# Hybrid decoder step on one core: the low part of the keys meets only the high part of the queries, two heads at a time

## The chip, the cores and the metric

The kernel runs on one core of one Trainium2 chip. The metric is the device time of one execution in microseconds (us); lower is better. Three executions of the kernel before took 1845.82, 1846.70 and 1847.45 us, so its median is 1846.7 us. Engines are called TensorE (PE in the profile, its weight loads PEld), VectorE (DVE), ScalarE (ACT), GpSimd (POOL) and SyncE (SP).

## The reference, cut to what matters

The reference is one layer of a decoder trunk for 1024 prompt tokens and 8 new tokens (1032 rows in all). All numbers are float32. The two steps that the change touches are these:

```
# the indexer, per 128-query block: 8 heads of 64, one shared key of 64
logits = einsum("bqhd,bld->bqhl", qi, ki_all)
score  = einsum("bqhl,bqh->bql", relu(logits), wi)
score  = where(key position <= query position, score, -inf)
idx    = top_k(score, 256)

# attention over the chosen keys: 16 query heads, 4 key groups, 64 wide
s = einsum("bqcgd,bqkcd->bqcgk", q, k[idx])
p = softmax(where(valid, s, -inf))
o = einsum("bqcgk,bqkcd->bqcgd", p, v[idx])
```

Ahead of them stand an RMS norm and one wide input projection; beside them a gated spatial unit; behind them an output projection, a squared-ReLU MLP and a gated embedding.

## The kernel before, in words

**High and low parts.** TensorE multiplies in a rounded float32 type, one pass for each matmul. To keep precision, an operand x is split into a high part (rounded) and a low part (the rest), and a product takes several matmuls that add up in the same place. Dense projections take three (high by high, high by low, low by high). Scores are done otherwise. A head is 64 wide and the array has 128 rows, so `split_heads` stacks a query head's high part and low part into the 128 rows: for an even head the high part lies in rows 0 to 63 and the low part in rows 64 to 127, for an odd head the other way round. The keys' high part is laid twice, in both halves of the rows (`kih` for the indexer, `khd[c]` for key group c of attention), and so is their low part (`kil`, `kld[c]`). One matmul with the high keys then gives (high + low query) by high key, and a second with the low keys gives (high + low query) by low key.

**Index scores.** `score_tiles` goes over the query tiles 2 to 7 (tile i sees L = 128 (i + 1) keys; tiles 0 and 1 need no choice). For each of the 8 heads it takes a room of two banks (`bank2`, there are two such rooms, used in turn, and other steps of that phase use them too), makes the logits in stretches of at most 512 keys, lets ScalarE take the relu out of it, and VectorE adds it with its weight to the tile's score. It is a generator: `tick`, called after each group of a dense projection, advances it by one step, that is one head for tiles 4 to 7 and two heads for tiles 2 and 3. So score matmuls stand between groups of 24 dense matmuls on TensorE's in-order queue. VectorE meanwhile picks the 256 best of finished tiles in the background (`take_tiles`, maximum of 8 and replace), which `pump` paces by modelled clocks.

**Attention.** 32 units (8 query tiles by 4 key groups, in the order of `units`: a long and a short tile alternate) are given as operations with an engine, a planned duration, dependencies and a priority (`Op`); `emit` plays them through with these durations and writes them to the engines' queues in the order that results. For a unit of L keys there are: scores on TensorE (tile "sc"; before, one operation for each head if L > 512, one for two heads otherwise, where the two heads share one room of two banks), a masked copy with the row's maximum on VectorE for each head (`masked`), the exponential on ScalarE, transposes of the probabilities on TensorE in steps of 128 keys (tile "pp"), their copy on ScalarE or VectorE, and the product with the values on TensorE (tile "po", two matmuls side by side on 64 columns of the array each). `s_used` keeps the last masked copy of each score operation; a score operation waits for the one before the last, whose room it takes over.

The change touches `score_tiles` and, within `unit_ops`, `scores` and the loop that makes the score operations. The planned duration of a score operation was 0.85 L + 15 ns for each head.

Of the kernel before, what the change touches and what calls it, by code (L numbers as in the profile page):

```python
# [16 lines left out]
P = 128  # L17
# [23 lines left out]
LAT, LAT2, SLACK, S_FIRST, T_LAST = 180.0, 60.0, 0.0, 1.5, 0.1  # L41
# [28 lines left out]
def step_kernel(ctx, tc, xT, pT, w_in, w_o, w_up, w_down, w_pg, w_p, gv, gqk, wsT, b_s,  # L70
# [35 lines left out]
    def slot(name, shape=(P, T), dt=F32):  # L106
        return big.tile(list(shape), dt, name=name, tag="s", bufs=NSLOT)
# [13 lines left out]
    def bank2(name):  # L121
        return ps.tile([P, 1024], F32, name=name, tag="big", bufs=2)

    mm = pe.matmul
# [222 lines left out]
    for k in range(KC):  # L347
        h, l = slot("xh", dt=F32R), slot("xl", dt=F32R)
# [25 lines left out]
    qis = [qis_all[:, h, :] for h in range(HI)]  # L374
# [68 lines left out]
    kih, kil = key_split  # L443
# [5 lines left out]
    def mask_tile(i):  # L449
        L = (i + 1) * P  # L450
        if i not in (2, 4):
            return slot("mask", [P, L])
        if not packs:
            packs[0] = slot("mask", [P, 1024])
        return packs[0][:, :L] if i == 2 else packs[0][:, 1024 - L:]

    def score_tiles(tiles):
        behind = None
        n = 0
        for i in tiles:  # L460
            L = (i + 1) * P
            mask[i] = m = mask_tile(i)
            for h in range(HI):
                p = bank2("lg")
                for a in range(0, L, 512):
                    b = min(L, a + 512)
                    mm(p[:, a:b], qis[h][:, i * P:(i + 1) * P], kih[:, a:b], start=True, stop=False)
                    mm(p[:, a:b], qis[h][:, i * P:(i + 1) * P], kil[:, a:b], start=False, stop=True)
                rl = slot("rl", [P, L])
                act.activation(rl, p[:, :L], AF.Relu)  # L470
                if behind:
                    behind()

                def behind(m=m, rl=rl, h=h, i=i, L=L):
                    if h == 0:
                        dve.tensor_scalar(m, rl, wi[:, i, h:h + 1], None, op0=ALU.mult)
                    else:
                        dve.scalar_tensor_tensor(out=m, in0=rl, scalar=wi[:, i, h:h + 1], in1=m,
                                                 op0=ALU.mult, op1=ALU.add)
                    if h == HI - 1:  # L480
                        pool.affine_select(out=m[:, L - P:], in_=m[:, L - P:], pattern=[[-1, P]],
                                           compare_op=ALU.is_ge, fill=FUTURE, base=0, channel_multiplier=1)
                        scored.add(i)
                n += 1
                if i > 3 or n % 2 == 0:
                    yield 1
        behind()
        yield 1
# [13 lines left out]
    def take_tiles(tiles):  # L502
# [12 lines left out]
        yield 1  # L515

    paced.append(score_tiles(range(2, NT)))
    pairs = [(a, a + 1) for a in range(2, NT, 2)]
    takers = {t: take_tiles(t) for t in pairs}
# [385 lines left out]
    khd, kld = {}, {}  # L905
# [8 lines left out]
    qsts = {}  # L914
# [102 lines left out]
    for a, b in GROUPS[NG:]:  # L1017
# [10 lines left out]
        def scaled(eng, a, b, rest):  # L1028
            rest["sg"] = part("sg")
            eng.tensor_tensor(out=rest["sg"], in0=rest["p"][:, :b - a], in1=R[:, a:b], op=ALU.mult)  # L1030

        def gate(eng, rest):
            eng.activation(rest["sg"], rest["sg"], AF.Tanh, scale=0.5)

        def times(eng, a, b, rest):
            eng.scalar_tensor_tensor(out=mx_last[:, a:b], in0=rest["sg"], scalar=1.0, in1=mx_last[:, a:b],
                                     op0=ALU.add, op1=ALU.mult)
# [3 lines left out]
        o = Op("DVE", 430.0, lambda e, a=a, b=b, rest=rest: scaled(e, a, b, rest), [prev], -9.0)  # L1041
        o = Op("ACT", 380.0, lambda e, rest=rest: gate(e, rest), [o], -9.0)
        o = Op("DVE", 430.0, lambda e, a=a, b=b, rest=rest: times(e, a, b, rest), [o], -9.0)
    gated_out = Op("Pool", 2300.0, lambda e: gate_out(NT - 1, u_last, mx_last), [o], -9.0)
    keys_ready = {0: None}
# [15 lines left out]
    units = [(order[n + h], c) for n in range(0, NT, 2) for c in range(HKV) for h in range(2)]  # L1061
    q_ops = {order[0]: [], order[1]: []}
    s_ops, s_used, t_ops, t_used, pv_ops, ends, lasts = [], [], [], [], [], [], []
    q_last = {}

    def query_ops(i, deps, prio):
# [2 lines left out]
    def unit_ops(n, i, c):  # L1069
        L = (i + 1) * P  # L1070
        cols = slice(i * P, (i + 1) * P)
        env = {"p": [], "pt": {}}
        per = 4 if L <= 256 else 2 if L <= 512 else 1
        prio = float(n)
        back2 = ends[n - 2] if n >= 2 else None
        back3 = ends[n - 3] if n >= 3 else None
        room = lasts[n - 3] if n >= 3 else None
# [5 lines left out]
        ld = Op("SP", 120.0, load, [back3, gated_out if c == HKV - 1 else None], prio, lag=3000.0)  # L1083

        def scores(eng, hs):
            room = bank2("sc")
            for n, h in enumerate(hs):
                p = env["sc", h] = room[:, 512 * n:] if n else room
                lhs = qsts[i][h % 2][:, 2 * c + h // 2, :]
                for a in range(0, L, 512):  # L1090
                    b = min(L, a + 512)
                    mm(p[:, a:b], lhs, khd[c][:, a:b], start=True, stop=False)
                    mm(p[:, a:b], lhs, kld[c][:, a:b], start=False, stop=True)

        def masked(eng, h):
            if h == 0:
                env["mx"], env["sum"] = small("mx4", [P, 8], bufs=4), small("sm4", [P, 4], bufs=4)
            if h % per == 0:
                env["room"] = slot("p", [P, per, L])
            s = env["room"][:, h % per, :]  # L1100
            env["p"].append(s)
            eng.tensor_tensor_reduce(out=s, in0=env["sc", h][:, :L], in1=mask[i], scale=1.0, scalar=FUTURE,
                                     op0=ALU.add, op1=ALU.max, accum_out=env["mx"][:, h:h + 1])

        def bias(eng, h):
            sc = s_q[:, 2 * c + h // 2, i, h % 2:h % 2 + 1]
            eng.scalar_tensor_tensor(out=env["mx"][:, 4 + h:5 + h], in0=env["mx"][:, h:h + 1], scalar=-1.0, in1=sc,
                                     op0=ALU.mult, op1=ALU.mult)

        def exponential(eng, h):  # L1110
            s = env["p"][h]
            sc = s_q[:, 2 * c + h // 2, i, h % 2:h % 2 + 1]
            eng.activation(s, s, AF.Exp, bias=env["mx"][:, 4 + h:5 + h], scale=sc, accum_out=env["sum"][:, h:h + 1])  # L1113

        exps = []
        some = 2 if L <= 512 else 1
        for h0 in range(0, 4, some):
            hs = range(h0, h0 + some)
            deps = q_ops[i] + [keys_ready[c], room, s_ops[-1] if s_ops else None,
                               s_used[-2] if len(s_used) >= 2 else None]  # L1120
            so = Op("PE", some * (0.85 * L + 15), lambda e, hs=hs: scores(e, hs), deps, prio - S_FIRST)
            s_ops.append(so)
            for h in hs:
                mo = Op("DVE", 1.06 * L + 60, lambda e, h=h: masked(e, h), [so, back3, taken.get(i)], prio)
                bo = Op("DVE", 75.0, lambda e, h=h: bias(e, h), [mo], prio)
                exps.append(Op("ACT", 1.06 * L + 240, lambda e, h=h: exponential(e, h), [bo], prio))
            s_used.append(mo)

        def inverse(eng):
            rc = small("rc4", [P, 4], bufs=2)  # L1130
            eng.reciprocal(rc, env["sum"])
            env["rx"] = small("rx", [P, 4, 64], bufs=1)
            eng.tensor_copy(env["rx"], rc.unsqueeze(2).to_broadcast([P, 4, 64]))
# [57 lines left out]
    for n, (i, c) in enumerate(units):  # L1191
        if i not in q_ops:
            query_ops(i, [lasts[n - 4]] if n >= 4 else [], n - 8.0)
        unit_ops(n, i, c)
# [195 lines left out]
    for f in range(FFB):  # L1390
        for j in range(2):
            row = 4 * j
            for q, c in enumerate((j, j + 2)):
                h = hw[:, row + q, :]
# [85 lines left out]
    for n, (f, o) in enumerate(steps):  # L1480
# [26 lines left out]
        a = Pair("pa", True)  # L1507
# [19 lines left out]
        c = Pair("pc", False)  # L1527
# [3 lines left out]
        b = Pair("pb", False)  # L1531
# [35 lines left out]
    for k in range(KC):  # L1567
        e = slot("e")
# [86 lines left out]
```

## Time and profile before

| | |
|---|---|
| median of three runs | 1846.7 us |
| the profiled execution | 1844.18 us |
| its span in the profile | 1842.5 us |
| TensorE busy, instructions | 1795.2 us, 12106 matmuls |
| VectorE busy | 1269.2 us |
| ScalarE busy | 703.6 us |
| GpSimd busy | 556.9 us |
| index scores (tile lg) | 160 matmuls, from 65.7 to 283.9 us |
| attention scores (tile sc) | 384 matmuls, from 680.5 to 905.6 us |

The profile is of one execution. A row of the timeline gives the start and the length of an instruction, or of several alike that follow each other. Matmuls overlap in the array: the length of one is longer than the distance to the next, so what a matmul costs in a stream is the distance between starts, called a step here. A weight load (PEld) belongs to each matmul. The form 128*128 ahead of the operand's shape is rows by columns of the array that the instruction uses. The end of a matmul is modelled.

### The profile page before, as it was taken

To read this page: it belongs to the slowest core of one execution; us is meant where nothing else is said; L and a number is where in the kernel's file an instruction comes from. 1 tells how busy PE (TensorE), PEld (TensorE's weight loads), DVE (VectorE), ACT (ScalarE), POOL (GpSimd) and SP (SyncE) were. 2 spreads that over 40 slices of the span, in tenths; PEclk is the share of its full clock that TensorE was granted. 3 is DMA by queue.
4 is the path that set the end of the run, shared out by engine and by line. 5 is a ranking of instruction groups with operands and counts; after the bars stand their busy time and mean duration, and the time that the engine had idled before them with its cause. 6 is when DMAs were issued, how large, how long until landed. Compare 5 with 4: busy or idle time off the path is not lost.

```text
span 1842.5 us, 30644 instructions
## 1 busy us (share of the span) xinstructions
PE 1795.2 (97%) x12106; PEld 1689.0 (92%) x12106; DVE 1269.2 (69%) x2330; ACT 703.6 (38%) x1248; POOL 556.9 (30%) x511
## 2 busy tenths in 40 slices
PE   8999989999999999999999999999999999999898
PEld 8998879999999996777699999999998999999798
DVE  7489978989977757777744455556564666767743
ACT  5554332145311127777722333333335211211521
POOL 4233354457332221101012212211132336632321
PEclk9999999999999999999999999999999999999999
DMA  4122132222222265133142365555645667754233
GB/s 173 52 103 104 58 111 85 98 93 91 75 71 91 81 162 124 41 87 98 43 162 97 116 213 207 207 207 210 213 163 189 257 257 293 259 210 172 102 114 117
DMA packets 127328, 258.32 MB, mean 140 GB/s; under 512 B 13192, under 2 KB 58128, under 8 KB 127184
## 3 DMA queue, kind: packets, MB, share of 16 engines
q1 hardware_dynamic: 124992, 251.63, 39.7%
q0 software_dynamic: 2048, 4.72, 0.9%
q8 instruction: 95, 1.56, 0.3%
q14 instruction: 49, 0.40, 0.1%
q10 hardware_dynamic: 144, 0.02, 0.0%
HBM read 166.32 MB, written 90.01 MB: 139 GB/s over the span
## 4 chain that ended last, share of the span: by engine, by line
PE 80%; DVE 7%; issue 4%; POOL 4%; ACT 3%; DMA 1%; SPq 0%; POOLq 0%; ACTq 0%; DVEq 0%
PE acc L64 51%; PE pa L64 4%; PE pd L64 4%; PE pc L64 4%; PE po L64 4%; PE sc L64 4%; PE pp L64 4%; DVE mask L64 2%; PE pb L64 2%; DVE m L64 1%; POOL wlo L196 1%; PE mix L64 1%; DVE qs L64 1%; DMA kib<-cache_ki,idx 1%; PE lg L64 1%
## 5 line engine op out<-in xcount | busy, mean ns | idle before, releaser
L64 PE MATMUL acc<-xh,whi 128*128 128x344 f32 (+1 forms) x1144 | 372.9, 329 | 3.4 <-DVE s_q L64 1.8
L64 PE MATMUL acc<-xh,wlo 128*128 128x344 f32 (+1 forms) x1144 | 365.1, 323 | 1.8 <-POOL r_x L271 1.1
L64 PE MATMUL acc<-xl,whi 128*128 128x344 f32 (+1 forms) x1144 | 365.0, 323 | 1.0 <-DVE xl L64 0.9
L64 PE MATMUL acc<-nh,whi 128*128 128x344 f32 x960 | 303.0, 321 | 1.1 <-ACT e L1348 1.1
L64 PE MATMUL acc<-nh,wlo 128*128 128x344 f32 x960 | 301.8, 320 | 0.0
L64 PE MATMUL acc<-nl,whi 128*128 128x344 f32 x960 | 301.5, 319 | 0.0
L64 PEld LDWEIGHTS acc<-xh,whi 128*128 128x128 f32 x1144 | 216.4, 190 | 12.1 <-issue 5.0
L64 PEld LDWEIGHTS acc<-xh,wlo 128*128 128x128 f32 x1144 | 216.0, 189 | 2.7 <-POOL r_x L271 1.5
L64 PEld LDWEIGHTS acc<-xl,whi 128*128 128x128 f32 x1144 | 216.4, 190 | 2.2 <-DVE xl L64 1.8
L64 PEld LDWEIGHTS acc<-nh,whi 128*128 128x128 f32 x960 | 179.3, 188 | 2.8 <-ACT e L1348 1.8
L64 PEld LDWEIGHTS acc<-nl,whi 128*128 128x128 f32 x960 | 179.5, 188 | 0.0
L64 PEld LDWEIGHTS acc<-nh,wlo 128*128 128x128 f32 x960 | 179.4, 188 | 0.0
L64 DVE MATCH_REPLACE8 mask<-m,mask 128x384 f32<-128x384 f32 (+2 forms) x192 | 166.6, 875 | 0.0
L196 POOL TENSOR_TENSOR wlo<-wraw,whi 128x1024 fp32r<-128x1024 f32 x47 | 113.5, 2415 | 157.7 <-ACT whi L195 96.6
L64 DVE MAX8 m<-mask 128x8 f32<-128x384 f32 (+2 forms) x192 | 161.0, 880 | 0.0
L64 DVE TENSOR_TENSOR hop<-hw,hop 128x516 fp32r<-128x516 f32 x112 | 90.3, 817 | 98.1 <-ACT hop L1302 98.0
L1399 POOL TENSOR_TENSOR hw<-z 128x344 f32<-128x344 f32 x96 | 72.9, 761 | 278.1 <-ACT z L1398 278.1
L1398 ACT ACTIVATE z<-z 128x344 f32<-128x344 f32 x96 | 47.0, 492 | 221.0 <-DVE z L64 221.0
L1113 ACT ACTIVATE p<-p,mx,s_q 128x1024 f32<-128x1024 f32 (+7 forms) x128 | 110.4, 865 | 22.6 <-DVE mx L64 21.9
L195 ACT CAST whi<-wraw 128x1024 fp32r<-128x1024 f32 x96 | 100.1, 1043 | 1.4 <-DMA wraw<-w_up 1.3
L64 DVE CUSTOM_DVE_ANT_0 p<-sc,mask 128x1024 f32<-128x1024 f32 (+5 forms) x96 | 83.5, 886 | 22.0 <-PE sc L64 20.9
L64 PE MATMUL sc<-kh,qst 128*128 128x512 f32 (+3 forms) x384 | 89.3, 361 | 2.4 <-DVE mx L64 2.4
(303 smaller groups left out, 3526.7 us busy)
## 6 DMA issues: line engine op xcount, KB each, us to landing
h_d<-hop SPq DMA_DIRECT2D x98, 516.0 KB, 3.1
hop<-h_d SPq DMA_DIRECT2D x98, 516.0 KB, 5.9
wraw<-w_in SPq DMA_DIRECT2D x48, 512.0 KB, 4.1
wraw<-w_up SPq DMA_DIRECT2D x32, 512.0 KB, 4.4
draw<-w_down SPq DMA_DIRECT2D x32, 512.0 KB, 5.4
q_d<-qs SPq DMA_DIRECT2D x16, 512.0 KB, 3.5
qst<-q_d SPq DMA_DIRECT2D x16, 512.0 KB, 5.6
x<-xT SPq DMA_DIRECT2D x15, 516.0 KB, 8.2
```

Source lines behind the costliest of these rows:

```text
L64: return fn(*args, **kw)
L195: act.copy(hi, raws[n])
L196: eng.tensor_tensor(out=lo, in0=raws[n], in1=hi.bitcast(F32), op=ALU.subtract)
L1113: eng.activation(s, s, AF.Exp, bias=env["mx"][:, 4 + h:5 + h], scale=sc, accum_out=env["sum"][:, h:h + 1])
L1398: act.activation(z, z, AF.Relu)
L1399: pool.tensor_tensor(out=h[:, a:b], in0=z, in1=z, op=ALU.mult)
```

## The change

A new helper `head_pair` makes the scores of two heads. It takes one room of two banks if L is at most 512 and both rooms otherwise. For each stretch of at most 512 keys it issues the two full matmuls with the high keys, one for each head. Then it issues two matmuls with the low keys that use 64 rows each: the even head's high part in rows 0 to 63, the odd head's high part in rows 64 to 127. The product of the queries' low part and the keys' low part is no longer made. `score_tiles` calls it at each even head and reads the second result at the odd head. In attention each score operation makes two heads at any L; one of more than 512 keys waits for the masked copies of both score operations before it, and one of at most 512 keys that follows a long one waits for that one's last masked copy too. The planned duration becomes 0.69 L + 15 ns for each head.

```diff
+    def head_pair(name, L, q, kh, kl):
+        room = bank2(name)
+        outs = [room, room[:, 512:] if L <= 512 else bank2(name)]
+        for a in range(0, L, 512):
+            b = min(L, a + 512)
+            for x in range(2):
+                mm(outs[x][:, a:b], q(x), kh[:, a:b], start=True, stop=False)
+            for x in range(2):
+                o = slice(64 * x, 64 * x + 64)
+                mm(outs[x][:, a:b], q(x)[o], kl[o, a:b], start=False, stop=True)
+        return outs
...
             for h in range(HI):
-                p = bank2("lg")
-                for a in range(0, L, 512):
-                    b = min(L, a + 512)
-                    mm(p[:, a:b], qis[h][:, i * P:(i + 1) * P], kih[:, a:b], start=True, stop=False)
-                    mm(p[:, a:b], qis[h][:, i * P:(i + 1) * P], kil[:, a:b], start=False, stop=True)
+                if h % 2 == 0:
+                    ps_ = head_pair("lg", L, lambda x: qis[h + x][:, i * P:(i + 1) * P], kih, kil)
+                p = ps_[h % 2]
...
+    both_rooms = []
...
         def scores(eng, hs):
-            room = bank2("sc")
-            for n, h in enumerate(hs):
-                p = env["sc", h] = room[:, 512 * n:] if n else room
-                lhs = qsts[i][h % 2][:, 2 * c + h // 2, :]
-                for a in range(0, L, 512):
-                    b = min(L, a + 512)
-                    mm(p[:, a:b], lhs, khd[c][:, a:b], start=True, stop=False)
-                    mm(p[:, a:b], lhs, kld[c][:, a:b], start=False, stop=True)
+            outs = head_pair("sc", L, lambda x: qsts[i][x][:, 2 * c + hs[0] // 2, :], khd[c], kld[c])
+            for h, p in zip(hs, outs):
+                env["sc", h] = p
...
-        some = 2 if L <= 512 else 1
-        for h0 in range(0, 4, some):
-            hs = range(h0, h0 + some)
-            deps = q_ops[i] + [keys_ready[c], room, s_ops[-1] if s_ops else None,
-                               s_used[-2] if len(s_used) >= 2 else None]
-            so = Op("PE", some * (0.85 * L + 15), lambda e, hs=hs: scores(e, hs), deps, prio - S_FIRST)
+        for h0 in range(0, 4, 2):
+            hs = range(h0, h0 + 2)
+            used = s_used[-2:] if L > 512 else s_used[-2:-1] + [u for u in s_used[-1:] if u in both_rooms]
+            deps = q_ops[i] + [keys_ready[c], room, s_ops[-1] if s_ops else None] + used
+            so = Op("PE", 2 * (0.69 * L + 15), lambda e, hs=hs: scores(e, hs), deps, prio - S_FIRST)
...
             s_used.append(mo)
+            if L > 512:
+                both_rooms.append(mo)
```

## Rows read from the trace of the kernel before

**Rows 1.** The page, busy time of TensorE: us, share of the span, instructions

```profile
PE 1795.2 (97%) x12106; PEld 1689.0 (92%) x12106; DVE 1269.2 (69%) x2330; ACT 703.6 (38%) x1248; POOL 556.9 (30%) x511
```

**Rows 2.** Windows: stretch, its length, busy us of each engine, clock, DMA share, GB/s

```profile
60.00:140.00 80.00, 79.64 (x513) 75.04 (x513) 58.30 (x112) 43.68 (x91) 22.91 (x15) 1.00 0.26 90
140.00:220.00 80.00, 72.98 (x459) 67.61 (x458) 78.62 (x168) 34.11 (x65) 28.67 (x17) 0.98 0.24 86
220.00:290.00 70.00, 60.99 (x357) 56.27 (x356) 54.11 (x97) 21.66 (x29) 39.86 (x48) 0.93 0.31 102
...
676.00:920.00 244.00, 238.88 (x1652) 170.57 (x1652) 183.48 (x568) 176.89 (x367) 26.04 (x35) 1.00 0.35 91
```

**Rows 3.** Waits (total us, times, longest) and groups of 676 to 912 us

```profile
DVE p L64 <- PE sc L64: 21.4, 30, 3.0
...
PEld sc L64 <- DVE mx L64: 4.8, 8, 1.6
...
L64 PE MATMUL sc<-kh,qst 128*128 128x512 f32 (+3 forms) x384 | 89.3, 361 | 2.4 <-DVE mx L64 2.4
L64 DVE CUSTOM_DVE_ANT_0 p<-sc,mask 128x1024 f32<-128x1024 f32 (+5 forms) x96 | 83.5, 886 | 22.0 <-PE sc L64 20.9 <-PE acc L64 0.7
```

**Rows 4.** Chain of waits, 640 to 960 us: start, us, what

```profile
709.05 0.93 PE sc L64 x4
...
739.68 0.63 PE sc L64 x4
...
814.71 0.70 PE sc L64 x4
...
851.94 0.82 PE sc L64 x4
```

**Rows 5.** Timeline of TensorE around 765.59 us: one, two and eight value matmuls

```profile
765.59 0.43 PE L64 MATMUL po<-pt,vt 128*64 128x256 f32 x1
...
765.59 0.44 PE L64 MATMUL po<-pt,vt 128*64 128x256 f32 x2
...
765.59 1.08 PE L64 MATMUL po<-pt,vt 128*64 128x256 f32 x8
```

**Rows 6.** Timeline of TensorE, 336.6 to 338.1 us: 64 rows between full matmuls

```profile
336.75 0.32 PE L64 MATMUL acc<-xh,wlo 128*128 128x344 f32 x1
337.00 0.70 PE L64 MATMUL dix<-dw,sel 64*128 64x257 f32 x2
...
338.04 0.32 PE L64 MATMUL acc<-xh,wlo 128*128 128x344 f32 x1
```

**Rows 7.** Timeline of TensorE, 384.5 to 385.5 us, and that tile's group

```profile
384.61 0.32 PE L64 MATMUL acc<-xh,wlo 128*128 128x344 f32 x1
384.76 1.03 PE L64 MATMUL dsc<-kb,zq 128*128 128x257 f32 x4
...
L64 PE MATMUL dsc<-kb,zq 128*128 128x257 f32 x32 | 8.4, 383 | 1.8 <-ACT kb L768 1.8
```

**Rows 8.** Timeline of TensorE, 60.8 to 62.3 us, and the last transpose's group

```profile
60.90 0.33 PE L64 MATMUL acc<-xh,wlo 128*128 128x388 f32 x1
61.16 0.77 PE L64 MATMUL wit<-ident,kraw 64*128 64x64 f32 x9
...
62.28 0.32 PE L64 MATMUL acc<-xh,wlo 128*128 128x344 f32 x1
...
L64 PE MATMUL wit<-ident,kraw 64*8 64x64 f32 x1 | 0.2, 216 | 0.0
```

**Rows 9.** Timeline of TensorE: the first and the last scores followed by values

```profile
694.90 1.18 PE L64 MATMUL sc<-kh,qst 128*128 128x512 f32 x4
696.01 0.87 PE L64 MATMUL po<-pt,vt 128*64 128x256 f32 x6
...
905.01 0.93 PE L64 MATMUL sc<-kh,qst 128*128 128x384 f32 x4 [0.15 <-DVE mx L64]
905.87 0.65 PE L64 MATMUL po<-pt,vt 128*64 128x256 f32 x4
```

**Rows 10.** Waits of 62 to 290 us: who waited for whom, total us, times, longest

```profile
PE lg L64 <- ACT rl L470: 7.0, 2, 5.0
...
PE hst L64 <- DVE qs L64: 4.5, 3, 1.7
```

## The prediction

> **What bounds the kernel now.** I read the shares of the page first. TensorE is busy for 97% of the span [rows 1], so any change of its work is suspect of moving the end. A busy share is a mean, so the windows come next, one for each stretch that the change touches [rows 2]. The index scores (tile "lg") lie between 60 and 290 us. From 60 to 140 us TensorE is busy 79.64 of 80 us and VectorE 58.30. From 140 to 220 us it is the other way round: VectorE 78.62, TensorE 72.98. From 220 to 290 us neither is full. The attention scores (tile "sc") lie in the stage from 676 to 920 us, where TensorE is busy 238.88 of 244 us, VectorE 183.48 and ScalarE 176.89. The groups and waits of that stage say the same: the 384 score matmuls are a large share of its TensorE time, VectorE waits 21.4 us in 30 waits for scores, and TensorE's weight loads wait 4.8 us in 8 waits for VectorE [rows 3]. So in the attention stage every microsecond of TensorE counts almost fully, in the index stage only partly.
>
> **What one step of a matmul costs.** The chain of waits shows runs of four score matmuls, two heads' worth of one pass pair, at four key lengths: 0.93 us at 1024 keys, 0.82 at 896, 0.70 at 768 and 0.63 at 640 [rows 4]. Each run is one head: two matmuls of 512 columns and two of the rest. So a step of 512 columns is 0.93/4 = 0.2325 us, and two of the rest cost 0.355, 0.235 and 0.165 us: 0.178 us a step at 384 columns, 0.118 at 256, 0.083 at 128. At 128 that is more than a quarter of the 512 step: there the weight load binds.
>
> **What goes.** Call a block what one pass of the new loop does: two heads, one stretch of up to 512 keys. Before, it is four full matmuls. After, it is two full ones, and two half ones, each on 64 of the array's 128 rows, meant to run side by side: the time of one. The number of instructions stays; one step a block goes, if the halves do run together. Attention: 4 key groups x 2 pairs x (one block for tiles 0 to 3, two for tiles 4 to 7) = 96 blocks, which fits the 384 matmuls of [rows 3]. 48 are 512 wide, 16 each 384, 256 and 128 wide: 48 x 0.2325 + 16 x (0.178 + 0.118 + 0.083) = 17.2 us. Index: 4 pairs of heads, tiles 2 to 7, 40 blocks, of which 24, 8, 4 and 4 have these widths: 5.6 + 1.4 + 0.5 + 0.3 = 7.8 us. The trace has no two halves by rows, but it has pairs by columns, the "po" matmuls on 64 of 128 columns: one takes 0.43 us, two together 0.44, and eight of 256 columns 1.08 us [rows 5], where eight one after another would take 8 x 0.217 = 1.74 (0.217 is the step of 257 such columns on the full array, below). So a second half costs some 0.01 us or less; I take 0.007: 136 x 0.007 = 1.0 us. Saved: 17.2 + 7.8 - 1.0 = 24.0 us.
>
> **What comes: changes of the array's shape.** Full matmuls and half ones now alternate in each block. The kernel before has two places where 64-row instructions with 128 columns stand between full ones. At the first, the full matmul before begins at 336.75, two passes of "sel" follow, and the third full one behind begins at 338.04: 1.29 us [rows 6]. Without a price for the change it would be one step of 0.16 (336.75's own), two passes, and two steps of 0.16. A pass of the same 257 columns and type on the full array takes 0.217 us: four of them take 1.03 us with the last one's 0.383 [rows 7]; and they begin 0.15 us after the full matmul ahead, so a change of type alone costs nothing. That makes 0.16 + 0.43 + 0.32 = 0.91; the other 0.38 us are two changes, 0.19 us each. At the second place nine small transposes on 64 rows stand between a matmul that begins at 60.90 and one, the third behind, at 62.28 [rows 8]. Nine in 0.77 us, the last one's 0.216 taken off, are steps of 0.069. So 0.18 + 9 x 0.069 + 0.32 = 1.12, which leaves 0.26 us or 0.13 a change, with a smaller operand to load. I take 0.19, since the half matmuls load 128 columns as "sel" does; bounds are 0 (no row shows these two types in this order) and 0.27 (0.19 plus one more 128-column step of 0.083, if the second half's weights load behind the first's). The Trainium skill's page "TensorEngine Tiling (Array Packing)", section "Tiling Modes", says that a change of tiling mode drains the engine, and gives no price; by that rule every block pays, and the trace's 0.19 us is what a drain and an uncovered weight load look like.
>
> How many changes? One into each block: 136. Out of a block: attention has 32 inside an operation (first to second block of a long tile) and 64 at its end. The end is free where a "po" run follows, since such a run is on 64 columns and pays for its own change today. 42 of the 78 score runs of before are followed so (first and last in [rows 9]); at that share 34 of 64 are free and 30 paid. 96 + 32 + 30 = 158 changes, 158 x 0.19 = 30.0 us, less 17.2 - 0.7 saved: attention **+13.5 us**. Bounds by the exits alone: 7.8 (all free) to 20. Index: 40 in, 40 out, about 5 free ahead of the four-column-strip sums: 75 x 0.19 = 14.3, less 7.8 - 0.3: **+6.8 us** of TensorE. The change would be even at 24.0 / 233 = 0.103 us a change.
>
> **What of it reaches the end.** Index: the last 8 blocks (tile 7) and the first 16 cost 1.4 and 2.7 us; the middle 16 (tiles 5, 6), 2.7 us, lie in the stretch that VectorE fills. There TensorE waited 4.5 us for VectorE's splits in 3 waits [rows 10]. A later TensorE finds these waits shorter, so I take 4 of the 5.4 us of the first 32 blocks as hidden. If that cover is gone, they count. Tile 7 runs where TensorE waited 7.0 us in 2 waits for ScalarE's relu to free a room [rows 10]. A pair now wants both rooms at once and asks one head earlier, so these waits begin sooner; the dense work behind moves after them, but the same ScalarE instructions end them. I take +1.5 us (0 to 5). Index: 6.8 - 4 + 1.5 = **+4.3 us**.
>
> Attention: pairs of more than 512 keys take both rooms too, and wait for both masked reads of the pair before (0.886 us mean for one [rows 3]). TensorE's queue is in order, so whatever the planner puts behind a waiting pair (transposes, values) waits along, and VectorE, which waits for scores already, starves. The planner can fill in: a long tile has 5 to 8 steps of transposes and values a unit for two pairs. I take +2 us (0 to 8). The planner's new prices (0.69 for 0.85 us per 1000 columns of a head, too low by my sum) reorder all queues, SP's loads too; plus or minus 4. Where TensorE already idles in that stage (5 us) some of the extra hides: -1. No transfer is moved by the code itself, and no other engine's work changes.
>
> Sum: 13.5 + 4.3 + 2 - 1 = **+18.8 us**. On the profiled execution's 1844.2 us (span 1842.5) that is 1863; the median of the runs shown is 2.5 us above it, so I forecast **1865 us**. Its own range is 1850 (0.13 a change: 14 us less, and 1 us of index left) to 1880 (exits paid, rooms at 8).
>
> **Rivals.**
> (1) The change of shape is cheap between these types, and TensorE gains. Against it stand both 64-row places [rows 6, 8]; for it, that they are of another type than the score matmuls and that there are only two. The planner's new price is 0.16 us less per 1000 columns of a head: 2 x 0.16 x 36.9 = 11.8 us in attention (sum of keys over 64 pairs 36,864) and, at that price, 2 x 0.16 x 16.9 = 5.4 in the index stage, of which half counts: 14.5 us gained, **1832 us**. It decides below 0.103 us a change.
> (2) No price at all. The skill's page "TensorE: Matmul & The Clock Gate", section "Part 3: Packing small matmuls", models a packed span as one matmul plus some 4 ns for each further tile, without any term for a change of shape. As a mechanism of this kernel: 16.5 us gained in attention, 5 in the index stage, **1825 us**; rows 6 and 8 speak against it.
> (3) The losses are covered: exits mostly into "po" runs, fewer such runs since there are fewer score operations, index hidden. Against it: TensorE's 238.88 of 244. **1847 us**.
> (4) Rooms. Each of the 32 long pairs waits for a whole masked read: 32 x 0.886 = 28 us at most, half of it 14 in place of my 2: **1878 us**. For it: both rooms held, VectorE at 75%. Against it: the filling work.
> (5) The halves do not run side by side. Then the 25.0 us saved are not, attention +17, index about +5 more: **1888 us**. Only column pairs speak against it [rows 5].
>
> **How the numbers follow.** Forecast 0.57; (1) 0.13; (2) 0.04; (3) 0.07; (4) 0.12; (5) 0.07. A measurement of this kernel tells about 0.2% (3.7 us) from no change. Faster: (1), (2) and a little of (3), 0.18. Within 0.2%: most of (3), 0.05. Slower: 0.77. The range leaves out (1) and (2) and what lies above (5): 1840 to 1888.
>
> **What would show it.** Timeline of TensorE within a block: the first half some 0.19 us late after the second full matmul (right if over 0.15, (1) if under 0.1); the two halves' starts under 0.02 us apart (else (5)); a full matmul behind a block again about 0.19 us late. The attention stage should last about 259 us in place of 244, with no more than some 10 us of TensorE waits for VectorE's masked reads (else (4)). The stretch from 140 to 220 us should show shorter waits for VectorE's splits. The prediction is wrong if the total is under 1843, or if the stage grows by waits and not by steps.

## The result, and the profile after

The changed kernel takes 1872.9 us (median of 4 runs, 1868.6 to 1874.8), the kernel before 1846.3 us beside it (4 runs, 1845.4 to 1847.5): a ratio of 1.014 with the interval 1.0121 to 1.016, so it is slower by 26.6 us. The forecast was 1865, the range 1840 to 1888. The profiled execution took 1871.6 us (span 1869.8), that of before 1844.2.

The page of the kernel after, busy time of each engine, answers to [rows 1]:

```profile
PE 1815.9 (97%) x12106; PEld 1665.9 (89%) x12106; DVE 1270.4 (68%) x2330; ACT 703.6 (38%) x1248; POOL 556.9 (30%) x511
```

As many instructions as before on every engine, and 20.7 us more of TensorE. The windows of the kernel after (stretch, length, busy us of TensorE, its weight loads, VectorE, ScalarE, GpSimd; then clock, DMA share, GB/s) say where. The first three answer to [rows 2]. The fourth is the attention stage, from the first score matmul to the first matmul that applies the output's high part ("acc" from "mh"); its ends move with the kernel. The fifth is the first 20 us of that stage.

```profile
60.00:140.00 80.00, 80.00 (x503) 70.45 (x502) 58.22 (x114) 42.50 (x88) 22.86 (x14) 1.00 0.25 90
140.00:220.00 80.00, 78.40 (x488) 67.76 (x487) 77.48 (x164) 35.79 (x69) 28.76 (x18) 1.00 0.26 93
220.00:290.00 70.00, 59.77 (x346) 51.94 (x345) 53.02 (x92) 21.07 (x28) 44.95 (x52) 0.93 0.28 99
...
680.00:946.00 266.00, 253.50 (x1627) 155.47 (x1625) 180.96 (x566) 176.27 (x366) 25.72 (x34) 0.97 0.30 79
680.00:700.00 20.00, 16.12 (x74) 10.74 (x73) 12.05 (x33) 10.51 (x21) 2.36 (x1) 0.83 1.00 255
```

The last two windows in the kernel before, with the stage between the same two matmuls:

```profile
680.00:920.00 240.00, 234.88 (x1627) 166.57 (x1627) 182.44 (x566) 176.40 (x366) 25.74 (x34) 1.00 0.34 88
680.00:700.00 20.00, 18.20 (x110) 14.55 (x109) 16.61 (x45) 13.74 (x27) 2.40 (x1) 1.00 0.87 220
```

What lies ahead of the stage takes as long as before: the first score matmul begins at 680.2 (680.5 before), although TensorE is busy 78.40 us in place of 72.98 between 140 and 220. The stage lasts 265.8 us (240.0): +25.8. From the end of the stage to the start of the last matmul it takes 918.3 (916.5). So nearly the whole loss is in the attention stage. There TensorE does as many matmuls in 18.6 us more of busy time, stands idle 12.5 us (5.1 before), and the granted clock is 0.97 (1.00). Apart from the first 20 us, two windows of the stage have a lower clock:

```profile
820.00:840.00 20.00, 18.93 (x114) 12.55 (x114) 13.71 (x51) 12.34 (x31) 1.46 (x2) 0.91 0.13 34
860.00:880.00 20.00, 19.10 (x110) 11.57 (x110) 14.03 (x45) 13.55 (x28) 1.69 (x3) 0.91 0.19 47
```

As an estimate from these rows, (0.17 + 0.09 + 0.09) x 20 us = 7 us of the stage's 25.8 are lost to the clock. The waits of that stage in the kernel after (total us, times, longest), to [rows 3]:

```profile
DVE p L64 <- PE sc L64: 44.2, 37, 2.9
...
PEld sc L64 <- issue: 34.7, 112, 0.7
...
PEld sc L64 <- DVE mx L64: 9.5, 16, 2.3
...
PE sc L64 <- DVE mx L64: 5.2, 8, 2.0
```

"Issue" means that the loads of the scores' weights waited for nothing that the profile shows: 112 times, 34.7 us (14 times, 5.4 us in the same stage of before, and 13 times, 5.8 us in e2 below, which has the order of after but one shape only). That is the change of shape. VectorE waits for scores twice as long as before. Waits of the scores for VectorE's last read of a room ("mx" follows the masked read) are a smaller part.

**One pair of 1024 keys, step by step.** The timeline of the weight loads in the kernel after, 722.2 to 724.6 us; a line is a run of one shape with its start, and the idle time ahead of it is in brackets:

```profile
722.24 0.30 PEld L64 LDWEIGHTS sc<-kh,qst 128*128 128x128 f32 x2 [0.39 <-DVE mx L64]
722.91 0.19 PEld L64 LDWEIGHTS sc<-kh,qst 64*128 64x128 f32 x2 [0.37 <-issue]
723.34 0.30 PEld L64 LDWEIGHTS sc<-kh,qst 128*128 128x128 f32 x2 [0.24 <-issue]
724.00 0.19 PEld L64 LDWEIGHTS sc<-kh,qst 64*128 64x128 f32 x2 [0.36 <-issue]
724.43 0.20 PEld L64 LDWEIGHTS po<-pt,vt 128*64 128x64 f32 x4 [0.24 <-issue]
```

Ahead of every change the loads stand idle for 0.24 to 0.37 us, where within a shape the second load lies beside the matmul ahead of it. From full loads to full loads a block lasts 1.10 us (722.24 to 723.34), the next 1.09, where four full matmuls took 0.93 [rows 4]. The forecast per block was three steps and two changes, 3 x 0.2325 + 2 x 0.19 = 1.08. The two halves run side by side: the records of the two matmuls start at 722.909 and 722.912. The timeline of TensorE just ahead of them (a narrow window, so that it ends with the first half) shows where the block's second full matmul starts:

```profile
722.58 0.83 PE L64 MATMUL sc<-kh,qst 128*128 128x512 f32 x2
```

So the steps are 0.34 us from full to full (722.24 to 722.58), 0.33 from full to half and 0.43 from half to full. Against a step of 0.2325 they are late by 0.11, 0.10 and 0.20 us: the price of the two changes, 0.40 us, is paid in three places.

**The stage's start.** The timeline of TensorE in the kernel after, 688 to 700 us:

```profile
688.20 0.32 PE L64 MATMUL acc<-xh,wlo 128*128 128x344 f32 x1
...
689.17 0.70 PE L64 MATMUL sc<-kh,qst 128*128 128x128 f32 x4 [0.65 <-DVE mx L64]
...
690.90 0.67 PE L64 MATMUL sc<-kh,qst 128*128 128x128 f32 x4 [1.03 <-DVE mx L64]
...
691.73 0.49 PE L64 MATMUL sc<-kh,qst 128*128 128x512 f32 x1 [0.16 <-DVE mx L64]
...
694.26 3.39 PE L64 MATMUL sc<-kh,qst 128*128 128x512 f32 x7 [2.04 <-DVE mx L64]
...
697.58 1.86 PE L64 MATMUL pp<-ident,p 128*128 128x128 f32 x8
```

The same of the kernel before:

```profile
691.93 0.32 PE L64 MATMUL acc<-xh,wlo 128*128 128x344 f32 x1
692.09 1.03 PE L64 MATMUL pp<-ident,p 128*128 128x128 f32 x8
```

The last projection matmuls ("acc"), which TensorE has as filling work here, end at 688.2 in place of 691.9: the order of after has 21 of them between the first two pairs of long heads, that of before 6. Then nothing is left, TensorE stands four times (0.65 + 1.03 + 0.16 + 2.04 us) for VectorE's reads, and the first eight transposes come 5.5 us later and take 1.86 us in place of 1.03: the granted clock is 0.50 from 697.6 to 699.2 us, the lower of its two levels (1.2 in place of 2.4 GHz), after an engine that stood and waited, and 1.00 from 692.1 to 693.0 us in before. The clock of 680 to 700 is 0.83.

### The profile page after: what moved, and what is told of

Same layout as the page of the kernel before. It is cut to its first block, busy times and chain, and to the rows that moved or that the text cites. A ratio compares the mean times of both kernels' runs of the same rounds, so it can differ in the third digit from the quotient of the medians.

```text
span 1869.8 us, 30638 instructions
## 1 busy us (share of the span) xinstructions
PE 1815.9 (97%) x12106; PEld 1665.9 (89%) x12106; DVE 1270.4 (68%) x2330; ACT 703.6 (38%) x1248; POOL 556.9 (30%) x511
## 5 line engine op out<-in xcount | busy, mean ns | idle before, releaser
L64 PEld LDWEIGHTS acc<-xh,whi 128*128 128x128 f32 x1144 | 215.3, 189 | 14.3 <-issue 6.2
L1121 ACT ACTIVATE p<-p,mx,s_q 128x1024 f32<-128x1024 f32 (+7 forms) x128 | 110.3, 865 | 13.9 <-DVE mx L64 12.8
L64 PE MATMUL sc<-kh,qst 128*128 128x512 f32 (+7 forms) x384 | 95.2, 423 | 5.5 <-DVE mx L64 5.2
```

The source lines that it names most:

```text
L64: return fn(*args, **kw)
```

## The experiments

Medians, each against the kernel before on the same chip; "stage" is the attention stage by the two matmuls named above, from the profiled execution. `head_pair` serves the index scores too, so e2 to e6 and e9 change both; the stage leaves the index scores out.

| run | us | ratio (interval) | stage |
|---|---|---|---|
| before | 1846.3 | 1 | 240.0 |
| after | 1872.9 | 1.014 (1.0121 to 1.016) | 265.8 |
| e1_index_only | 1845.2 | 0.9986 (0.9976 to 0.9995) | 239.8 |
| e2_four_full | 1858.6 | 1.0057 (1.0039 to 1.0075) | 253.9 |
| e3_three_full | 1841.2 | 0.9967 (0.9955 to 0.9979) | 241.9 |
| e4_fulls_first | 1857.0 | 1.0056 (1.0034 to 1.0078) | 251.5 |
| e5_full_old_price | 1860.3 | 1.0069 (1.0052 to 1.0086) | 256.8 |
| e6_true_price | 1871.4 | 1.0134 (1.0109 to 1.0159) | 266.1 |
| e7_short_only | 1848.8 | 1.0009 (1.0 to 1.0019) | 242.1 |
| e8_index_fulls_first | 1845.5 | 0.9999 (0.9989 to 1.0008) | 239.8 |
| e9_full_by_head | 1857.0 | 1.005 (1.0034 to 1.0067) | 253.7 |
| e10_one_room | 1855.6 | 1.0041 (1.0027 to 1.0054) | 251.0 |

**e1_index_only**: head_pair in the index scores alone; the attention part of before.

```diff
-            outs = head_pair("sc", L, lambda x: qsts[i][x][:, 2 * c + hs[0] // 2, :], khd[c], kld[c])
+            room = bank2("sc")
+            for n, h in enumerate(hs):
...
```

> Only the index scores are made by pairs with half matmuls; attention is as before. Theory A (the index stage hides its extra work behind VectorE and ScalarE, all of the loss is in attention): 1846 us, within 2 us of before, first attention score within 1 us of before. Rival, my prediction's own term: 1850 us (+4.3). If the index stage were the cause of half the loss: 1859 us.

Measured: 1845.2, 0.14% below the kernel before. The window of e1 from 140 to 220 us:

```profile
140.00:220.00 80.00, 78.37 (x488) 67.73 (x487) 77.49 (x161) 35.37 (x68) 28.67 (x17) 1.00 0.26 93
```

The extra work of TensorE is there (78.37 us for 72.98 in [rows 2]) and costs nothing: VectorE fills this stretch in both, and TensorE had 7 us of room.

**e2_four_full**: the changed kernel, with the low pass by two full matmuls again. Order, rooms and planned price are those of after, the shapes those of before.

```diff
-                mm(outs[x][:, a:b], q(x)[o], kl[o, a:b], start=False, stop=True)
+                mm(outs[x][:, a:b], q(x), kl[:, a:b], start=False, stop=True)
```

> The changed kernel with its pairs, rooms and planned durations, but the low pass is made by two full matmuls with the whole query, as before: no change of the array's shape, as many steps as before. Theory A (some 14 us of the 25.8 us that the attention stage grew are changes of shape less the steps saved, the rest is rooms and the new order): 1857 us. Rival B (rooms and order are nearly all of it): 1870 us. Rival C (changes of shape are all of it, and the waits of the changed kernel only follow from them): 1847 us.

Measured: 1858.6, 14.3 us below after and 12 above before. So the loss has two parts of about the same size: the changes of shape net of the steps saved, and everything else in the rewrite (11.9 and 13.9 us of the stage). The windows of e2, the stage and its first 20 us:

```profile
679.00:933.00 254.00, 240.62 (x1627) 169.12 (x1625) 180.90 (x566) 176.14 (x366) 25.73 (x34) 0.99 0.32 83
680.00:700.00 20.00, 16.26 (x85) 13.06 (x84) 13.50 (x38) 12.23 (x24) 2.37 (x1) 0.83 1.00 248
```

The same matmuls as in before take 5.7 us more of busy time (240.62 for 234.88), and TensorE stands 13.4 us in place of 5.1. The weak start is there without any change of shape. Behind the first 20 us the stage's clock is 1.00, so the clock makes some 0.17 x 20 = 3.4 of the 5.7 us, an estimate.

**e3_three_full**: each block three full matmuls, without a change; the low pass of the second head is left out of the computation.

```diff
-            for x in range(2):
-                mm(outs[x][:, a:b], q(x), kh[:, a:b], start=True, stop=False)
-            for x in range(2):
-                o = slice(64 * x, 64 * x + 64)
-                mm(outs[x][:, a:b], q(x)[o], kl[o, a:b], start=False, stop=True)
+            mm(outs[0][:, a:b], q(0), kh[:, a:b], start=True, stop=False)
+            mm(outs[1][:, a:b], q(1), kh[:, a:b], start=True, stop=True)
+            mm(outs[0][:, a:b], q(0), kl[:, a:b], start=False, stop=True)
```

> As the run with four full matmuls, but the second head's low pass is left out (its scores lack that part): three steps in a block and no change of shape, what the change would cost if the array changed shape for nothing. Theory A: 1857 - 16 = 1841 us. Rival B: 1855 us, the steps give little back because rooms bind. Rival C: 1830 us.

Measured: 1841.2. This has the number of steps that the change aims at, but no change of shape; what lies between it and after is the price of the changes, 31.7 us (23.9 in the stage). And e2 to e3 is what the saved steps are worth: 17.4 us in both places together, of which 12.0 are in the stage, for steps of 17.2 there. Even at that best the rewrite ends only 0.33% below before: the order takes back most of what the steps give.

**e4_fulls_first**: a pair of more than 512 keys does the full matmuls of both blocks, then the four halves: 64 changes fewer in attention. It also takes 32 away in the index scores, which e8 shows to be worth nothing.

```diff
-        for a in range(0, L, 512):
-            b = min(L, a + 512)
+        parts = [(a, min(L, a + 512)) for a in range(0, L, 512)]
+        for a, b in parts:
             for x in range(2):
                 mm(outs[x][:, a:b], q(x), kh[:, a:b], start=True, stop=False)
+        for a, b in parts:
             for x in range(2):
```

> The changed kernel, but a pair of more than 512 keys makes the full matmuls of both its blocks first and then the four half ones: two changes of shape fewer in each of the 32 long pairs of attention, 64 x 0.2 us = 12.8 us of TensorE. Theory A: 1873 - 12.8 = 1860 us. Rival B (the stage waits for rooms): 1869 us or more. Rival C (each change also starves VectorE): 1856 us or less.

Measured: 1857.0, 15.9 us below after (14.3 in the stage): 0.22 to 0.25 us for each change taken away. A pair in the timeline of e4's weight loads, now with one change in and one out:

```profile
680.62 0.80 PEld L64 LDWEIGHTS sc<-kh,qst 128*128 128x128 f32 x4
...
681.79 0.30 PEld L64 LDWEIGHTS sc<-kh,qst 64*128 64x128 f32 x4 [0.37 <-issue]
...
682.45 0.19 PEld L64 LDWEIGHTS acc<-xh,whi 128*128 128x128 f32 x1 [0.37 <-issue]
```

It takes 1.83 us from 680.62 to the next work; the same pair in after starts at 680.05 and hands over at 682.28: 2.23. That is 0.20 us for each of the two changes.

**e5_full_old_price** and **e6_true_price**: is the 12 us of e2 the planner's price? e5 is e2 with before's price of 0.85; e6 is after with a price near what a block takes.

```diff
-            so = Op("PE", 2 * (0.69 * L + 15), lambda e, hs=hs: scores(e, hs), deps, prio - S_FIRST)
+            so = Op("PE", 2 * (0.85 * L + 15), lambda e, hs=hs: scores(e, hs), deps, prio - S_FIRST)
```

```diff
-            so = Op("PE", 2 * (0.69 * L + 15), lambda e, hs=hs: scores(e, hs), deps, prio - S_FIRST)
+            so = Op("PE", sum(3 * ((min(L, a + 512) - a) / 2.4 + 16) + 400 for a in range(0, L, 512)), lambda e, hs=hs: scores(e, hs), deps, prio - S_FIRST)
```

> As the run with four full matmuls (1858.6 us, 12 above before), but each head's planned duration is 0.85 L + 15 ns again, which is what four full steps take. Theory P (the 12 us come from an order planned with scores that are too cheap): 1848 us. Theory Q (they come from the long pairs holding both rooms, so that scores wait for two masked copies): 1858 us.

> The changed kernel with the planned duration that its own blocks take in the trace: three steps and 0.4 us for two changes of shape in each block (2.17 us for a pair at 1024 keys, where it plans 1.44). Theory P: 1865 us or less. Theory Q: 1872 us.

Measured: 1860.3 against e2's 1858.6, and 1871.4 against after's 1872.9. Neither price matters; that theory falls.

**e7_short_only**: halves only in attention tiles of up to 512 keys, which are pairs already in before. Order, rooms and prices are before's; the long tiles and the index scores as before.

```diff
+            if len(hs) == 2:
+                outs = head_pair("sc", L, lambda x: qsts[i][x][:, 2 * c + hs[0] // 2, :], khd[c], kld[c])
+                for h, p in zip(hs, outs):
+                    env["sc", h] = p
+                return
...
```

> Half matmuls only in attention and only for tiles of at most 512 keys; the order of all queues, the rooms and the planned durations are those of before. 32 blocks lose one step (4.9 us) and gain 32 changes of shape into them and some 15 out of them (47 x 0.2 = 9.4 us). Theory A (a change of shape costs 0.2 us on the path): 1846.5 + 4.5 = 1851 us. Rival: the stage's waits take it up, 1847 us.

Measured: +2.5 us. With the 4.9 us of steps saved and the 47 changes counted in its expectation, (2.5 + 4.9) / 47 = 0.16 us a change: a small loss (its interval begins at 1.0) even without a new order or new rooms. It holds for the four lengths together; which of them lose was not measured.

**e8_index_fulls_first**: e4's order in the index scores, attention of before.

> Half matmuls only in the index scores (that run took 1845.2 us, 0.14% below before), with the full matmuls of both blocks of a long tile ahead of the half ones: 16 long pairs with two changes of shape fewer, 6.4 us of TensorE. If the stage is bound by VectorE and ScalarE as theory A has it: 1844 us, 0 to 2 us below the index-only run. If TensorE bound it: 1839 us.

Measured: 1845.5 against e1's 1845.2, overlapping: fewer changes bring nothing where TensorE doesn't set the end.

**e9_full_by_head**: e5 with the first head's matmuls ahead of all of the second's, so that the first masked read can begin half a pair earlier (shown against after, without the line of the planned duration).

```diff
-        for a in range(0, L, 512):
-            b = min(L, a + 512)
-            for x in range(2):
+        for x in range(2):
+            for a in range(0, L, 512):
+                b = min(L, a + 512)
                 mm(outs[x][:, a:b], q(x), kh[:, a:b], start=True, stop=False)
-            for x in range(2):
-                o = slice(64 * x, 64 * x + 64)
-                mm(outs[x][:, a:b], q(x)[o], kl[o, a:b], start=False, stop=True)
+                mm(outs[x][:, a:b], q(x), kl[:, a:b], start=False, stop=True)
```

> As the run with four full matmuls and the old planned duration (1860.3 us), but within a pair the first head's matmuls are all issued before the second's, so that the first needs only the room whose masked copy ended a read earlier. The plan and the order of the queues are unchanged. Theory Q1 (TensorE itself stands and waits for the second room): 1853 us, a saved read of some 0.9 us in a part of the 32 long pairs. Theory Q2 (the coarser operations and their dependencies make a worse order, no matter which room is free): 1860 us.

Measured: 1857.0, 3.3 us below e5 with overlapping intervals: at most a small part. The waits of e9's stage:

```profile
DVE p L64 <- PE sc L64: 17.2, 21, 2.7
...
PEld sc L64 <- DVE mx L64: 4.5, 9, 1.2
...
PE sc L64 <- DVE mx L64: 3.7, 6, 1.3
```

VectorE now waits less for scores than in [rows 3] (17.2 us for 21.4), and the kernel is still 0.5% slower than before. A wait table tells who waited, not what the time went on.

**e10_one_room**: the kernel before, one head at a time, four full matmuls; only the plan is told that a long score operation needs the last masked read done too, as a pair that holds both rooms does.

```diff
-                               s_used[-2] if len(s_used) >= 2 else None]
+                               s_used[-2] if len(s_used) >= 2 else None,
+                               s_used[-1] if s_used and L > 512 else None]
```

> The kernel before, one head at a time, with one dependency more in the plan: a score operation of more than 512 keys also waits for the last masked copy, as the changed kernel's pairs do. The rooms on the chip are as before, so nothing new can be waited for there except through the order. Theory Q1: 1848 us. Theory Q2: 1855 us or more, the order alone costs the larger part of the 12 us.

Measured: 1855.6 (1849.5 to 1858.8), 9.4 us above before, where e2 is 12 above. No pair, no half, no other room: the order that this dependency makes is enough to cost that. It holds back each of 64 single heads here and each of 32 pairs in e2, so the 9.4 us are not simply a part of the 12. The windows of e10, the stage (it begins at 684.3 here) and its first 20 us:

```profile
684.30:935.30 251.00, 239.02 (x1626) 169.78 (x1624) 183.53 (x569) 176.58 (x363) 25.77 (x34) 0.99 0.32 84
684.30:704.30 20.00, 17.75 (x93) 14.65 (x92) 13.86 (x40) 13.16 (x25) 2.38 (x1) 0.83 1.04 265
```

It is the same kind of weak start: the clock is 0.83, and the first transposes come 13.2 us after the first score matmul, 17.4 in after and 11.6 in before. The idle time in the stage is that of after, too (12.0 us). Its nine executions say what goes with it: the three with a mean granted clock of 0.994 to 0.996 took 1849.5 to 1852.1 us, the six with 0.988 to 0.991 took 1852.8 to 1858.8. So much of what this order costs comes together with a lower clock.

## Why the prediction was right, and where it was wrong

- **Slower, because changes of shape cost more than the step saves: right.** A block lasts 1.10 us for 1.08 forecast. After less e2 is +14.3 us (11.9 in the stage), for 13.5 in the sum. With the 16.5 saved, the stage gives 28.4 / 158 = 0.18 us a change, for 0.19. 36 of the 64 exits fall into value runs; 34 were forecast. In the stage of other runs a change costs 0.22 (e4) and 0.15 us (e3, 23.9 over 158), and by its whole time 0.16 in e7. A lower clock is in these figures: by the rows of the windows after loses some 3.6 us more to it than e2, and 1.8 more than e3 and e4. So rivals (1) and (2) fall, and (3) with them, since the loss is not covered. The Trainium skill's page "TensorEngine Tiling (Array Packing)", section "Tiling Modes", has the drain, and the loads' idle time here (0.24 to 0.37 us) agrees with it; the span model of "TensorE: Matmul & The Clock Gate", section "Part 3: Packing small matmuls", has no term for it, and by that model after would have come out below before.
- **The halves run as one: right** (3 ns between the starts). Rival (5) falls.
- **Index stage +4.3: wrong.** All of it is hidden: e1 measures -1.6 us. (The attention stage starts 0.3 us earlier in after, but a single profile is no measure of that: with the index scores of before it starts at 680.5, in e7 at 682.6 and in e10 at 684.3.) I hid 4 us of the 6.8 under VectorE and charged the rest and 1.5 for rooms. VectorE sets the pace between 140 and 220 us, and the waits of TensorE for VectorE's splits [rows 10] are gone from the list. The wait for ScalarE's relu stays as it was, 6.8 us for 7.0.
- **Rooms and order in attention +2 (0 to 8), replanning plus or minus 4: the terms that were mis-sized.** They measure +12 (e2), outside the first bound and at the end of both together. I looked for a price in waits on the chip, and took the plan's filling for granted. The runs show that an order alone can cost that much: e10, with nothing but a dependency in the plan, is 9.4 us slower, while planned prices (e5, e6) and the moment at which a room comes free (e9) have little or nothing. Rival (4) had the right place and about the right size (14 for 12), but the waits that it counted are a small part: those of the score matmuls for masked reads grew from 2.4 us [rows 3] to 5.5 in e2's stage.
- **Where TensorE idles, 1 us of the extra hides: wrong.** Idle time in the stage grew from 5.1 to 12.5 us.
- **The tests named.** The block's length and the halves came out as said, the places within the block did not: the first half is 0.10 us late, where over 0.15 was to be right and under 0.1 was to be (1), the full matmul behind 0.20, and the second full one 0.11, which had no place in the tests. The stage was to last about 259 in place of 244 by the wide window: it grew by 25.8. Waits of the scores for VectorE's reads are 9.5 us by their loads and 5.2 by their matmuls, and the second lie within the first, so they stay under the limit of 10 and do not speak for (4). The sum came out 7.8 us low, by +10 in attention's order against +4.3 in the index stage; the rest is within what single profiles tell. That the time lies so near the forecast is in part luck, since these two misses have opposite signs. Two slips of its working change nothing: a run of four score matmuls in [rows 4] is one head and not two heads' worth, and the index stage's 6.8 us are shared out by blocks alone, where its own steps and changes give tile 7 some 1.1 us and not 1.4.

Open: how e2's 12 us divide. Its rows show 8.3 us more idle and 5.7 more busy time for the same matmuls in the stage, and the lower clock of the first 20 us makes some 3.4 of the busy part; no run held the clock and changed the order. Nor was the second new dependency (of a short operation behind a long pair) tried by itself. That e4 gives more for each change than e3 and e7 is not explained in full: e4's changes all lie inside a pair, where the trace shows 0.20 us each, and the others have the exits too.

## What to carry to other kernels

Halving an operand's rows to run two matmuls side by side saves one step of 0.23 us at 512 columns and here pays about 0.2 us on each way in and out of the other shape, so group all matmuls of one shape first (e4 got 16 us back that way), and count the changes before the steps. An operation that is made larger also waits for more: give the planner only that new dependency, with the old code (e10), and see what the order costs before building the rest. Extra work of TensorE cost nothing in a stretch that VectorE fills (e1), so read the price of an edit from its own stretch and not from the page's 97%.

## What the runs showed of the hardware that was not expected

Two VectorE operations on one column, which take 0.28 us together elsewhere in the stage, took 2.19 us at 691.6 in the kernel after. The timeline of VectorE there, and a normal pair behind it:

```profile
691.59 2.19 DVE L64 SCALAR_TENSOR_TENSOR mx<-mx,s_q 128x1 f32<-128x1 f32 x2
...
694.12 0.28 DVE L64 SCALAR_TENSOR_TENSOR mx<-mx,s_q 128x1 f32<-128x1 f32 x2
```

GpSimd's timeline has a product of 1032 columns over the same time:

```profile
691.33 2.36 POOL L957 TENSOR_TENSOR u<-u,mx 128x1032 f32<-128x1032 f32 x1 [15.32 <-DVE mx L64]
```

VectorE's operations end as the product ends (693.78 and 693.69). All twelve traces show it at this last product of 1032 columns: in each, VectorE's work on "mx" or its copy "rx", which takes 0.3 us elsewhere, begins under the product and ends 0.1 to 0.2 us behind it (in before the copy "rx", 1.65 us at 695.76). The rounds of picking under the earlier products (MATCH_REPLACE8, 1.2 us) do not: they end before the product does. That one holds up the other was not tried. If so, it is part of the 2.04 us that TensorE stood at that place in after, and of 1.86 us in e2, where the same two operations take 2.20 us. In before the stretched copy costs VectorE 1.4 us too, but later in the stage. So a part of the weak start of the pairs may be this, and not the wait for rooms.
